# Hybrid layer with attention and pooling: pooling channels in another order, inputs of embedding, heads and gates asked for at other products, pooling operands made in two groups

## The chip, the cores and the metric

The kernel runs on one core of a Trainium2 chip. The metric is the time of one execution on the device in microseconds (us); lower is better. An execution is profiled by the hardware, and the profile's span leaves out a little at the start and the end. The engines are PE (matrix products), DVE (vector), ACT (scalar, activations), POOL and SP; SP, ACT and POOL also ask for transfers (DMA), each in its own order.

## What is computed

One decoder layer over 1024 tokens of width 2048, in f32. A projection gives queries, keys, values, two gates and the pooling channels. Sliding-window attention with 16 heads and a multi-scale pooling mixer are each multiplied by a SiLU gate, joined, and sent through one output projection. A gated embedding of p is added before the norm.

```
h = jnp.einsum('bsd,dc->bsc', x, w_in) + b_in
q, k, v, g_attn, u_pool, g_pool = jnp.split(h, SPLIT_POINTS, axis=-1)
a = banded_sink_attention(q, k, v, sinks, bias_hqk, valid) * jax.nn.silu(g_attn)
b = multiscale_pool(u_pool, w_pool, pool_scale) * jax.nn.silu(g_pool)
mix = jnp.einsum('bsc,cd->bsd', jnp.concatenate([a, b], axis=-1), w_out)
ple = jax.nn.sigmoid(jnp.einsum('bsd,de->bse', x, w_gate_ple)) * jnp.einsum('bsp,pd->bsd', p_i, w_ple)
return layer_norm(DEEPNORM_ALPHA * x + mix + ple, ln_gain, ln_bias)
```

The pooling has four channel groups 0 to 3, with trailing windows of 2, 4, 8 and 16 tokens: the mean over the window, less the token, then a 256 x 256 map per group (w_pool) and a scale.

## The kernel before

**Products.** A job is two blocks of 128 output columns over 1024 tokens. It is worked out by seven products in place of eight (p1 to p7, Strassen's way), on sums and differences of quarters of the weight and of the token operand. Every f32 operand is split into a high and a low part, and mm3 (L176) makes three matmuls of each step: high by high, high by low, low by high. A product is four such steps, 12 matmuls of 128 x 512. Weights arrive raw by SP (`raw`, a ring of five), DVE makes the sums, ACT casts the high part (L222, `wh`), DVE subtracts for the low part (`wl`), four products ahead of their use. The operand of the tokens (`b11`, `b21`, `t1` to `t4`, `b22`, each with an h and an l tile) is made once per stage by split_unit (L240: ACT L248, then DVE). Results leave the two banks qa and qb of PSUM by an ACT copy (L346) or a DVE add into `part`. Slots of a rotating pool (`s`) hold what is fetched beside.

**Stages.** s1 and s2 are the first and second half of the inner width for query, key and value columns, and s2 goes on with all others, whose partial sums go to memory. s3 takes the other half of the width for these others: gate and pooling channel pairs (gp, u) in turn, one attention gate pair, eight pairs of the embedding's gate (wgate), three attention gate pairs. s4 multiplies the pooled half by w_out, s5 the attended half, s6 the last 256 tokens. In each stage the first two and the last two jobs run side by side, products in turn (BESIDE, 14 products), the others alone (ALONE, 7 products).

**What sets the order.** A tick is one product. `after(n, fn)` (L155) writes fn's instructions into the program n ticks on, `later(n, fn)` the same but also behind the last marked result of PE, ACT or DVE. The order on each engine is therefore the order in which the program writes, and each engine and each of the DMA queues of SP, ACT and POOL takes its instructions in that order.

**What the change touches.**
- heads (L473): one head and token half per 9 ticks beside s2's products. begin fetches the query and the bias (SP), split makes the query's parts (ACT L485, L487, DVE), score makes the scores (PE L506), then softmax, share, value, shift and trans.
- pool_u (L608): window sums of a channel block by doubling, on DVE: 1, 2, 3 or 4 adds per half for groups 0 to 3, with a scalar_tensor_tensor and a split behind. After the second block it fetches the group's w_pool and the pooling gates (sgp), and mix (L640) makes 24 matmuls into banks sc, multiplied on DVE (L652) and stored by POOL to cc.
- embed_in (L656) fetches four tiles of p one per two ticks, and splits them after nine (ACT L668, DVE); embed_w (L672) fetches a pair of w_ple and splits it (ACT L150).
- gate_ahead (L592) fetches the attention result `pre` of a gate block, gate_attn (L595) applies silu and multiplies.
- set_from (L255) makes a stage's token operands from memory: begin and each step ask for tiles `two` (ACT's queue, L267), and step i makes operand i, the first as b11, b21, t1, t2 and so on.

Of the kernel before, what the change touches and what calls it, by code (L numbers as in the profile page):

```python
# [32 lines left out]
T = 512  # L33
# [7 lines left out]
Q0, KB, VB, GA0, U0, GP0 = 0, 8, 9, 10, 18, 26  # L41
# [22 lines left out]
class Layer:  # L64
# [405 lines left out]
    def heads(self, h, j):  # L470
        nc, g = self.nc, j // 4
# [21 lines left out]
        def score(bq):  # L493
            sc[bq] = self.slot()[:, :T].rearrange("p (e k) -> p e k", e=2)
            ps = self.bank("sc", 2, (P, 2, 256))
            z = k0(bq)

            if bq:
                win = [(h, (bq - 1) * P, 0, 2 * P)]
            else:  # L500
                win = ([(0, 3 * P, 0, P)] if h else []) + [(h, 0, P, P)]
            for e in range(2):
                q = qs[e][:, bq * P : (bq + 1) * P]
                for hh, o, at, n in win:
                    for i, kk in enumerate(self.kk[hh]):
                        nc.tensor.matmul(ps[:, e, at : at + n], q, kk[:, o : o + n], start=i == 0, stop=i == 1)  # L506
            for e in range(2):
                nc.vector.tensor_tensor_reduce(
                    out=sc[bq][:, e, z:], in0=ps[:, e, z:], in1=bias[0][:, e, z:], op0=ALU.add, op1=ALU.max, scale=1.0,
                    scalar=self.c(C_SINK + 8 * j + 2 * bq + e), accum_out=mx[:, 2 * bq + e : 2 * bq + e + 1])  # L510

        def shift(bq):
            f = slice(2 * bq, 2 * bq + 4)
            nc.vector.tensor_scalar(out=neg[:, f], in0=mx[:, f], scalar1=-1.0, scalar2=None, op0=ALU.mult)
            self.tt(sk[:, f], self.c(C_SINK + 8 * j + 2 * bq, 4), neg[:, f], ALU.add)
            nc.scalar.activation(sk[:, f], sk[:, f], AF.Exp)
# [14 lines left out]
        def share(bq):  # L531
            cur = sc[bq][:, :, P:]
            for e in range(2):
                i = 2 * bq + e
                nc.scalar.activation(cur[:, e], cur[:, e], AF.Copy, scale=rec[:, i : i + 1])
# [44 lines left out]
        self.later(3, split)  # L580
        for bq in range(4):
            t = 4 * (bq // 2)
            self.after(4 + 2 * bq, lambda bq=bq: score(bq))
            if bq % 2:
                self.after(8 + t, lambda bq=bq: shift(bq - 1))
                self.after(14 + t, lambda bq=bq: trans(bq - 1))
            self.after(9 + t, lambda bq=bq: softmax(bq))
            self.later(11 + t, lambda bq=bq: share(bq))
            self.after(19 + t + bq % 2, lambda bq=bq: value(bq))


    def gate_ahead(self, j):  # L592
# [15 lines left out]
    def pool_u(self, j, c):  # L608
        nc, g = self.nc, j // 2
        w = 2 << g  # L610
        out = []
        for h in range(2):
            u = self.slot()
            if h == 0:
                nc.gpsimd.memset(u[:, 0:16], 0.0)
            else:
                self.ident_act(u[:, 0:16], c[:, 0, T - 16 :], self.c(C_BIN + U0 + j))
            self.ident_act(u[:, 16:], c[:, h], self.c(C_BIN + U0 + j))
            cur, d, first = u, 1, 1
            while d < w:  # L620
                nxt = self.slot()
                end = 2 * d == w
                f = 16 if end else first
                self.tt(nxt[:, f:], cur[:, f:], cur[:, f - d : T + 16 - d], ALU.add)
                cur, d = nxt, 2 * d
                first = first + d
            if h == 0:
                self.tt(cur[:, 16 : 16 + 16], cur[:, 16 : 16 + 16], self.c(C_HEAD + 16 * g, 16), ALU.mult, nc.gpsimd)
            nc.vector.scalar_tensor_tensor(out=cur[:, 16:], in0=cur[:, 16:], scalar=1.0 / w, in1=u[:, 16:],
                                           op0=ALU.mult, op1=ALU.subtract)  # L630
            out.append(self.split(cur[:, 16:], 2 * (j % 2) + h < 3))
        self.diff[j] = out
        if j % 2:
            f = slice((g % 2) * T, (g % 2) * T + T)
            self.after(4, lambda: self.got.update({("wp", g): self.fetch(self.wpool[g // 2][:, f])}))
            self.later(8, lambda: self.got.update({("wp", g): self.split(self.got["wp", g])}))
            self.after(8, lambda: self.got.update({("sg", g): [[self.fetch(self.sgp[2 * g + e][:, h * T : h * T + T]) for e in range(2)] for h in range(2)]}))
            self.later(10, lambda: self.mix(g))

    def mix(self, g):  # L640
# [183 lines left out]
    def run(self):  # L824
# [23 lines left out]
        win, wgate, wout = self.win, self.wgate, self.wout  # L848
        pairs = lambda b, n: [(b + 2 * i, b + 2 * i + 1) for i in range(n)]
# [2 lines left out]
        store = lambda w: hid if w is win else gat  # L852
        qkv = [(win, *p) for p in [(KB, VB)] + pairs(Q0, 4)]
        ga, gp, u = ([(win, *p) for p in pairs(b, 4)] for b in (GA0, GP0, U0))
        rest = [j for two in zip(gp, u) for j in two] + ga[:1] + [(wgate, *p) for p in pairs(0, 8)] + ga[1:]

        def keep(where):
            return lambda b, c: self.load(where[b], flat(c))
# [52 lines left out]
        n2, n3, n4, n5 = (len(s) - 2 for s in (s2, s3, s4, s5))  # L911
# [81 lines left out]
        self.after(5, lambda: build_kv(KB, self.k_build, 0))  # L993
        self.after(6, lambda: build_kv(VB, self.v_build, 0))
        for i in range(16):
            self.after(t - 1 + 9 * i, lambda i=i: self.heads(i % 2, i // 2))
        self.after(t + 63 + 8, lambda: build_kv(KB, self.k_build, 1))
        self.after(t + 63 + 22, lambda: build_kv(VB, self.v_build, 1))
        self.centre_weights(8, 3)
# [9 lines left out]
        for i in range(n3):  # L1009
            if i == 1:  # L1010
                over.close()
                over = ExitStack()
                self.extras = self.work_pool("e2", 6, over)
            if self.groups[g + i + 1][0][0].b[0] == 0 and i < n3 - 1:
                self.after(1, self.embed_in)
                self.after(4, lambda: self.embed_w(0))
            if i == n3 - 1:

                over.close()
                work.close()  # L1020
                work = ExitStack()
                self.slot_n = T
                self.slots = self.work_pool("slots1", 6, work)
                self.twos = self.work_pool("twos1", 8, work)
                pooled()
                for n, b in enumerate(b for j in s3[-2:] for b in j.b):
                    self.after(4 + n, lambda b=b: self.gate_ahead(b - GA0))
            self.run_group(g + i, () if i else steps)
        g += n3

# [33 lines left out]
        for i in range(n4):  # L1064
            if i == 1:
                work.close()
                work = ExitStack()
                self.twos = self.work_pool("twos2", 8, work)
                p6.extend(5 * [pp] + [self.work_pool("p6", 1, work)])
                d0 = self.work_pool("d0", 4, work)  # L1070
            if i == n4 - 2:
                attended()
            self.run_group(g + i, () if i else make_pooled, renew if i == n4 - 1 else None)
        g += n4


# [134 lines left out]
```

## Time and profile before

| | us |
|---|---|
| median of 3 runs | 1502.66 (1502.1 to 1507.54) |
| the profiled execution | 1504.51 |
| its span | 1502.8 |
| PE busy in the span | 1453.8 (97%) |
| DVE, ACT, POOL busy | 1119.7, 781.1, 278.9 |

Lines of the profile read: L179 is line 179 of the kernel; in a row of the timeline stand start, length, engine, line, operation, what is written `<-` what is read, the shape, a count, and in brackets how long the engine was idle before and what released it. In a list of waits stand the engine and what waited, what it waited for, the time in all, how often, and the longest. The mean granted clock of PE over the execution was 0.989.

### The profile page before, as it was taken

Reading aid. Unit: us, or ns where it says so; the run is one execution under the profiler, and the core shown is the slowest. Engines: PE = TensorE matmul, PEld = TensorE weight load, DVE = VectorE, ACT = ScalarE, POOL = GpSimd, SP = SyncE. Lnnn points to the kernel's source line nnn. Section 1 sums busy time; section 2 is a strip of 40 time slices with the busy share of each in tenths; the row PEclk is TensorE's granted clock in tenths of the full one; section 3 lists DMA queues with packets and bytes.
Section 4 is the critical chain, followed back from the end, with each engine's and each line's share of the span. In section 5 each row is a group of like instructions: output and inputs, shape, how many; then the busy total and the mean of one; then the engine's idle time right before and its main releaser. Section 6 shows DMA issues by size and latency. Waiting matters only on the chain. (4 is left out here: it accounts for less than half of the span.)

```text
span 1502.8 us, 20461 instructions
## 1 busy us (share of the span) xinstructions
PE 1453.8 (97%) x6972; PEld 1225.5 (82%) x6972; DVE 1119.7 (75%) x2030; ACT 781.1 (52%) x1550; POOL 278.9 (19%) x388
## 2 busy tenths in 40 slices
PE   8999999999999999999999998999998999999986
PEld 6788888888878888888887786888886888899985
DVE  7788678888787877888675695556558866987785
ACT  5464566666666656566633353333337433555484
POOL 0000123332333332231111111000001111111241
PEclk9999999999999999999999999999999999999998
DMA  7563875445445555557766667575768678586564
GB/s 262 202 218 101 250 208 178 140 167 174 166 168 176 174 193 180 172 182 245 189 158 175 180 155 240 160 207 160 206 189 270 150 193 236 140 239 134 153 230 143
DMA packets 101721, 280.38 MB, mean 187 GB/s; under 512 B 11632, under 2 KB 16880, under 8 KB 101616
## 3 DMA queue, kind: packets, MB, share of 16 engines
q1 hardware_dynamic: 76400, 199.89, 39.9%
q0 software_dynamic: 19712, 67.64, 19.6%
q10 hardware_dynamic: 5504, 11.54, 2.3%
q8 instruction: 55, 0.90, 0.2%
q14 instruction: 50, 0.41, 0.1%
HBM read 193.04 MB, written 85.98 MB: 186 GB/s over the span
## 5 line engine op out<-in xcount | busy, mean ns | idle before, releaser
L222 ACT CAST wh<-raw 128x512 fp32r<-128x512 f32 x428 | 264.1, 620 | 450.8 <-PE qa L180 143.2
L122 DVE TENSOR_TENSOR wl<-raw,wh 128x512 fp32r<-128x512 f32 x428 | 298.2, 702 | 141.4 <-ACT wh L222 138.5
L346 ACT COPY part<-qa 128x512 f32<-128x512 f32 (+1 forms) x180 | 103.9, 577 | 54.0 <-PE qa L181 53.0
L551 POOL TENSOR_SCALAR_AFFINE_SELECT s<-s 128x512 fp32r<-128x512 f32 x128 | 101.0, 801 | 150.5 <-ACT s L544 101.1
L122 DVE TENSOR_TENSOR part<-part,qb 128x512 f32<-128x512 f32 (+1 forms) x120 | 81.0, 675 | 50.5 <-PE qb L181 47.0
L179 PE MATMUL qa<-b11h,wh 128*128 128x512 f32 (+2 forms) x292 | 110.7, 380 | 2.0 <-ACT b11h L248 1.7
L180 PE MATMUL qa<-b11l,wh 128*128 128x512 f32 (+2 forms) x292 | 109.5, 375 | 0.2 <-DVE b11l L122 0.2
L181 PE MATMUL qa<-b11h,wl 128*128 128x512 f32 (+2 forms) x292 | 109.0, 374 | 0.4 <-DVE wl L122 0.4
L179 PE MATMUL qb<-b21h,wh 128*128 128x512 f32 (+2 forms) x292 | 109.3, 374 | 0.0
L181 PE MATMUL qb<-b21h,wl 128*128 128x512 f32 (+2 forms) x292 | 108.9, 373 | 0.0
L180 PE MATMUL qb<-b21l,wh 128*128 128x512 f32 (+2 forms) x292 | 108.7, 372 | 0.0
L179 PE MATMUL qb<-t1h,wh 128*128 128x512 f32 (+1 forms) x260 | 102.1, 393 | 4.3 <-DVE part L122 2.9
L179 PE MATMUL qa<-t2h,wh 128*128 128x512 f32 (+1 forms) x260 | 100.6, 388 | 3.5 <-ACT wh L222 3.5
L179 PE MATMUL qa<-t3h,wh 128*128 128x512 f32 (+1 forms) x260 | 100.9, 388 | 3.1 <-ACT part L346 3.1
L181 PE MATMUL qb<-t1h,wl 128*128 128x512 f32 (+1 forms) x260 | 101.1, 389 | 1.5 <-DVE wl L122 1.5
L181 PE MATMUL qa<-t2h,wl 128*128 128x512 f32 (+1 forms) x260 | 100.0, 385 | 1.5 <-DVE wl L122 1.5
L180 PE MATMUL qb<-t1l,wh 128*128 128x512 f32 (+1 forms) x260 | 100.9, 388 | 0.0
L179 PE MATMUL qa<-t4h,wh 128*128 128x512 f32 (+1 forms) x260 | 100.4, 386 | 0.3 <-DVE part L122 0.3
L179 PE MATMUL qb<-b22h,wh 128*128 128x512 f32 (+1 forms) x260 | 100.4, 386 | 0.0
L180 PE MATMUL qa<-t4l,wh 128*128 128x512 f32 (+1 forms) x260 | 99.7, 383 | 0.0
L181 PE MATMUL qa<-t4h,wl 128*128 128x512 f32 (+1 forms) x260 | 99.7, 383 | 0.0
L180 PE MATMUL qa<-t3l,wh 128*128 128x512 f32 (+1 forms) x260 | 99.7, 383 | 0.0
(286 smaller groups left out, 3568.9 us busy)
## 6 DMA issues: line engine op xcount, KB each, us to landing
raw<-in_win SPq DMA_DIRECT2D x65, 512.0 KB, 4.2
h<-part SPq DMA_DIRECT2D x34, 512.0 KB, 2.9
part<-h POOLq DMA_DIRECT2D x34, 512.0 KB, 6.0
cw<-in_wout SPq DMA_DIRECT2D x64, 256.0 KB, 3.1
raw<-in_wgate SPq DMA_DIRECT2D x32, 512.0 KB, 4.1
raw<-wc SPq DMA_DIRECT2D x32, 512.0 KB, 4.4
s<-in_x SPq DMA_DIRECT2D x44, 256.0 KB, 5.3
wc<-cw SPq DMA_DIRECT2D x32, 256.0 KB, 2.3
```

Source lines behind the costliest of these rows:

```text
L122: return (eng or self.nc.vector).tensor_tensor(out=out, in0=a, in1=b, op=op)
L179: mm(ps, wh, xh, start=start, stop=False, skip_group_check=True)
L180: mm(ps, wh, xl, start=False, stop=False, skip_group_check=True)
L181: return mm(ps, wl, xh, start=False, stop=stop, skip_group_check=True)
L222: self.unit_latest = [nc.scalar.copy(out=hi, in_=src).ins, L.lo(lo, src, hi).ins]
L346: self.mark("ACT", self.nc.scalar.copy(out=dst, in_=ps))
L551: nc.gpsimd.affine_select(out=o4, in_=a4, pattern=[[0, 4], [sign, P]], compare_op=ALU.is_ge, fill=0.0, base=0 if side else -1, channel_mul ...
```

## The change

Five things move, and no instruction changes its kind or size. The heads begin one tick earlier, and all their steps but the fetch and the split keep their place. The pooling groups follow each other as 0, 3, 2, 1 in place of 0, 1, 2, 3, and the pooling gates are fetched two ticks earlier. The four fetches of p begin four ticks later, the first w_ple three ticks later. The pooling operands of s4 are made in s3's last group from tick 10 on, every second tick, in place of s4's first group; the stage's first job needs them from tick 14 on. The `pre` of the last gates are fetched from tick 9 in place of tick 4. In the changed kernel the lines from L1027 on have numbers higher by two.

```diff
--- before.py
+++ after.py
@@ -580,13 +580,13 @@
         self.later(3, split)
         for bq in range(4):
             t = 4 * (bq // 2)
-            self.after(4 + 2 * bq, lambda bq=bq: score(bq))
+            self.after(5 + 2 * bq, lambda bq=bq: score(bq))
             if bq % 2:
-                self.after(8 + t, lambda bq=bq: shift(bq - 1))
-                self.after(14 + t, lambda bq=bq: trans(bq - 1))
-            self.after(9 + t, lambda bq=bq: softmax(bq))
-            self.later(11 + t, lambda bq=bq: share(bq))
-            self.after(19 + t + bq % 2, lambda bq=bq: value(bq))
+                self.after(9 + t, lambda bq=bq: shift(bq - 1))
+                self.after(15 + t, lambda bq=bq: trans(bq - 1))
+            self.after(10 + t, lambda bq=bq: softmax(bq))
+            self.later(12 + t, lambda bq=bq: share(bq))
+            self.after(20 + t + bq % 2, lambda bq=bq: value(bq))
 
 
     def gate_ahead(self, j):
@@ -634,7 +634,7 @@
             f = slice((g % 2) * T, (g % 2) * T + T)
             self.after(4, lambda: self.got.update({("wp", g): self.fetch(self.wpool[g // 2][:, f])}))
             self.later(8, lambda: self.got.update({("wp", g): self.split(self.got["wp", g])}))
-            self.after(8, lambda: self.got.update({("sg", g): [[self.fetch(self.sgp[2 * g + e][:, h * T : h * T + T]) for e in range(2)] for h in range(2)]}))
+            self.after(6, lambda: self.got.update({("sg", g): [[self.fetch(self.sgp[2 * g + e][:, h * T : h * T + T]) for e in range(2)] for h in range(2)]}))
             self.later(10, lambda: self.mix(g))
 
     def mix(self, g):
@@ -852,7 +852,7 @@
         store = lambda w: hid if w is win else gat
         qkv = [(win, *p) for p in [(KB, VB)] + pairs(Q0, 4)]
         ga, gp, u = ([(win, *p) for p in pairs(b, 4)] for b in (GA0, GP0, U0))
-        rest = [j for two in zip(gp, u) for j in two] + ga[:1] + [(wgate, *p) for p in pairs(0, 8)] + ga[1:]
+        rest = [j for two in ((gp[g], u[g]) for g in (0, 3, 2, 1)) for j in two] + ga[:1] + [(wgate, *p) for p in pairs(0, 8)] + ga[1:]
 
         def keep(where):
             return lambda b, c: self.load(where[b], flat(c))
@@ -993,7 +993,7 @@
         self.after(5, lambda: build_kv(KB, self.k_build, 0))
         self.after(6, lambda: build_kv(VB, self.v_build, 0))
         for i in range(16):
-            self.after(t - 1 + 9 * i, lambda i=i: self.heads(i % 2, i // 2))
+            self.after(t - 2 + 9 * i, lambda i=i: self.heads(i % 2, i // 2))
         self.after(t + 63 + 8, lambda: build_kv(KB, self.k_build, 1))
         self.after(t + 63 + 22, lambda: build_kv(VB, self.v_build, 1))
         self.centre_weights(8, 3)
@@ -1012,8 +1012,8 @@
                 over = ExitStack()
                 self.extras = self.work_pool("e2", 6, over)
             if self.groups[g + i + 1][0][0].b[0] == 0 and i < n3 - 1:
-                self.after(1, self.embed_in)
-                self.after(4, lambda: self.embed_w(0))
+                self.after(5, self.embed_in)
+                self.after(7, lambda: self.embed_w(0))
             if i == n3 - 1:
 
                 over.close()
@@ -1023,8 +1023,10 @@
                 self.slots = self.work_pool("slots1", 6, work)
                 self.twos = self.work_pool("twos1", 8, work)
                 pooled()
+                for n, step in enumerate(make_pooled):
+                    self.after(10 + 2 * n, step)
                 for n, b in enumerate(b for j in s3[-2:] for b in j.b):
-                    self.after(4 + n, lambda b=b: self.gate_ahead(b - GA0))
+                    self.after(9 + n, lambda b=b: self.gate_ahead(b - GA0))
             self.run_group(g + i, () if i else steps)
         g += n3
 
@@ -1070,7 +1072,7 @@
                 d0 = self.work_pool("d0", 4, work)
             if i == n4 - 2:
                 attended()
-            self.run_group(g + i, () if i else make_pooled, renew if i == n4 - 1 else None)
+            self.run_group(g + i, then=renew if i == n4 - 1 else None)
         g += n4
```

The order on three queues shows it. First the heads, on DVE: at a head in s2, the rows about the low parts of the query (`s` of 64x512; `wl` are low parts of weights). Before:

```order
L122 TENSOR_TENSOR s_4492<-pv_4451,s_4493 64x256 x2
L122 TENSOR_TENSOR wl_4504<-s_915_4464,wh_4503 128x512
L122 TENSOR_TENSOR wl_4535<-raw_4064,wh_4534 128x512
L122 TENSOR_TENSOR s_4528<-s_4402,s_4528 64x512
L122 TENSOR_TENSOR s_4529<-s_4402,s_4529 64x512
L122 TENSOR_TENSOR st_4066<-st_4066 128x2
L122 TENSOR_TENSOR part_4501<-part_4501,qb_4538 128x512
```

and now:

```order
L122 TENSOR_TENSOR s_4492<-pv_4451,s_4493 64x256 x2
L122 TENSOR_TENSOR s_4501<-s_4374,s_4501 64x512
L122 TENSOR_TENSOR s_4502<-s_4374,s_4502 64x512
L122 TENSOR_TENSOR wl_4510<-s_915_4464,wh_4509 128x512
L122 TENSOR_TENSOR wl_4535<-raw_4069,wh_4534 128x512
L122 TENSOR_TENSOR st_4036<-st_4036 128x2
L525 RECIPROCAL st_4036<-st_4036 128x2
```

The two query rows stood behind the two weight rows, and now stand ahead of them.

Second the queue of SP at the passage from the pooling channels to the gates of the embedding (`raw` are gate weights, `in_p` and `in_wple` the embedding's inputs, `pre` the attention result, `in_wpool` the last pooling group's weight). Before:

```order
L136 DMA raw_8592<-in_wgate 128x1024
L136 DMA raw_8678<-in_wgate 128x1024
L136 DMA raw_8815<-in_wgate 128x1024
L136 DMA raw_8859<-in_wgate 128x1024
L136 DMA s_8680<-in_wple 128x512
L136 DMA s_8682<-in_p 128x512
L136 DMA s_8718<-in_p 128x512
L136 DMA s_8747<-pre_154 128x512
L136 DMA s_8749<-pre_154 128x512
L136 DMA s_8752<-pre_155 128x512
L136 DMA s_8754<-pre_155 128x512
L136 DMA s_8756<-in_wpool 128x512
```

and now:

```order
L136 DMA raw_8606<-in_wgate 128x1024
L136 DMA raw_8676<-in_wgate 128x1024
L136 DMA s_8712<-in_p 128x512
L136 DMA s_8737<-pre_154 128x512
L136 DMA s_8739<-pre_154 128x512
L136 DMA s_8742<-pre_155 128x512
L136 DMA s_8744<-pre_155 128x512
L136 DMA s_8746<-in_wple 128x512
L136 DMA s_8748<-in_wpool 128x512
L136 DMA s_8770<-in_p 128x512
L136 DMA s_8790<-sgp_164 128x512
L136 DMA s_8792<-sgp_165 128x512
```

Before, four loads of raw weights stand ahead of in_wple, in_wpool and the second in_p (the first in_p stands ahead of them all); now two do, and the others come behind.

Third DVE where s3 ends and s4 begins (`two`, `t1l`, `t2l` are pooling operands, `raw`, `s`, `wl` weights, `part<-s` the attention result times its gate, and `part<-qb` the add that frees a bank of PSUM). Before, the last 12 rows up to that add:

```order
L122 TENSOR_TENSOR raw_10680<-raw_10375,raw_10680 128x512
L122 TENSOR_TENSOR wl_10844<-s_2129_10838,wh_10843 128x512
L122 TENSOR_TENSOR raw_10375<-s_2129_10838,raw_10375 128x512
L122 TENSOR_TENSOR part_10484<-s_10586,part_10484 128x512
L122 TENSOR_TENSOR part_10484<-s_10588,part_10484 128x512
L122 TENSOR_TENSOR part_10485<-s_10612,part_10485 128x512
L122 TENSOR_TENSOR part_10485<-s_10614,part_10485 128x512
L122 TENSOR_TENSOR raw_10375<-raw_10375 128x512
L122 TENSOR_TENSOR two_10506<-two_10655,two_10506 128x1024
L122 TENSOR_TENSOR two_10507<-two_10656,two_10507 128x1024
L122 TENSOR_TENSOR s_2135_10877<-raw_10718 128x512
L122 TENSOR_TENSOR part_10794<-part_10794,qb_10886 128x512
```

and now:

```order
L122 TENSOR_TENSOR wl_10852<-s_2131_10846,wh_10851 128x512
L122 TENSOR_TENSOR raw_10375<-s_2131_10846,raw_10375 128x512
L122 TENSOR_TENSOR t2l_10870<-two_10507,t2h_10869 128x1024
L122 TENSOR_TENSOR raw_10375<-raw_10375 128x512
L122 TENSOR_TENSOR two_10604<-two_10643,two_10604 128x1024
L122 TENSOR_TENSOR two_10605<-two_10644,two_10605 128x1024
L122 TENSOR_TENSOR part_10486<-s_10737,part_10486 128x512
L122 TENSOR_TENSOR part_10486<-s_10739,part_10486 128x512
L122 TENSOR_TENSOR part_10487<-s_10766,part_10487 128x512
L122 TENSOR_TENSOR part_10487<-s_10768,part_10487 128x512
L122 TENSOR_TENSOR s_2137_10885<-raw_10706 128x512
L122 TENSOR_TENSOR part_10816<-part_10816,qb_10894 128x512
```

Before, the gate products of part_10484 and part_10485 and one pair of differences stand in the rows ahead of the add; now t2l, a further pair of differences and the gate products of part_10486 and part_10487 stand ahead of it as well, which came behind it before. From the first `b11l` to this add there are 28 rows before and 36 now.

## The prediction

> **What bounds the kernel now.** I read the page first, for the span and the busy shares.
>
> ```profile
> span 1502.8 us, 20461 instructions
> PE 1453.8 (97%) x6972; PEld 1225.5 (82%) x6972; DVE 1119.7 (75%) x2030; ACT 781.1 (52%) x1550; POOL 278.9 (19%) x388
> ```
>
> PE is busy for 1453.8 of 1502.8 us, so all its idle time is 49 us, and the change removes no matmul. It can only shorten or lengthen those 49 us, and the stretches in which PE runs at a lower granted clock. The list of waits, filtered to PE, says whom PE waits for: the time in all, how often, the longest.
>
> ```profile
> PE sc L179 <- ACT s L150: 5.3, 1, 5.3
> PE sc L506 <- DVE s L122: 5.2, 11, 1.2
> PE qa L179 <- ACT part L346: 3.1, 1, 3.1
> PE qb L179 <- DVE part L122: 2.9, 3, 1.0
> ```
>
> One wait at a pooling product is 5.3 us, eleven at head scores are 5.2 together, and one at a product of the last group is 3.1. A table of windows then shows where busy time (the first pair: length, PE busy) and the granted clock (the column before the DMA share) fall off.
>
> ```profile
> 450.00:500.00 50.00, 49.32 (x249) 41.19 (x249) 40.72 (x99) 29.71 (x76) 17.27 (x22) 1.00 0.55 181
> 900.00:950.00 50.00, 44.72 (x183) 36.13 (x182) 28.41 (x44) 18.14 (x28) 4.66 (x8) 0.93 0.72 222
> 1100.00:1150.00 50.00, 46.91 (x207) 38.43 (x206) 33.82 (x48) 25.29 (x37) 6.37 (x8) 1.00 0.83 247
> 1150.00:1200.00 50.00, 46.61 (x196) 37.56 (x195) 44.10 (x59) 25.54 (x38) 7.52 (x12) 0.97 0.60 158
> ```
>
> The heads lose little per window; 900 to 950 (the passage from pooling to gates) and 1100 to 1200 (the last s3 group and the first s4 group) lose most, and two of them lose clock too. The change works at these three places, in the order of the queues.
>
> **1. Heads one tick earlier.** Every head's score stays where it was among the products; its query fetch and split move one tick forward. The timeline of one head, PE first, then DVE:
>
> ```profile
> 448.60 0.33 PE L506 MATMUL sc<-kh,s 128*128 128x128 f32 x1 [1.21 <-DVE s L122]
> 446.06 0.69 DVE L122 TENSOR_TENSOR wl<-s,wh 128x512 fp32r<-128x512 f32 x1 [0.84 <-ACT wh L222]
> 446.68 0.69 DVE L122 TENSOR_TENSOR wl<-raw,wh 128x512 fp32r<-128x512 f32 x1
> 447.86 1.40 DVE L122 TENSOR_TENSOR s<-s,s 64x512 fp32r<-64x512 f32 x2 [0.49 <-ACT s L485]
> ```
>
> The two low parts of the query stand behind two weight splits on DVE; in the new order they stand ahead of them (rows above, in the section on the change). That is 2 x 0.6 us sooner, where the wait was 1.21. The weight splits that go back are for products further on, so PE does not wait there. The order moves low parts past a weight split in 10 of the 16 heads, so I take 10/16 of 5.2: **-3.3** (from -1 to -5.2).
>
> **2. Embedding inputs asked for later, pooling order 0, 3, 2, 1.** The 5.3 us wait, by engine: PE, ACT, then SP.
>
> ```profile
> 907.43 0.80 PE L179 MATMUL sc<-e,s 128*128 128x512 f32 x1 [5.28 <-ACT s L150]
> 906.24 0.62 ACT L668 CAST s<-s 128x512 fp32r<-128x512 f32 x1 [6.33 <-DMA s<-in_p]
> 906.76 0.61 ACT L150 CAST s<-s 128x512 fp32r<-128x512 f32 x1
> 862.08 26.69 SPq L136 DMA_DIRECT2D raw<-in_wgate  x4
> 864.57 0.33 SPq L136 DMA_DIRECT2D raw<-in_wgate  x1
> 889.33 0.86 SPq L136 DMA_DIRECT2D s<-in_p  x2
> 890.29 2.15 SPq L136 DMA_DIRECT2D s<-pre  x4
> 893.30 0.33 SPq L136 DMA_DIRECT2D s<-in_wpool  x1
> ```
>
> The pooling weight's cast (906.76) is what PE waits for, but ACT had stood 6.33 us before the embedding input's cast ahead of it, and that input was asked for at 889.33. SP had been held since 864.57 behind raw gate weights that wait for buffers, with wple, p, pre and wpool queued behind. PE's loss goes on after the gap:
>
> ```profile
> 906.80:913.60 6.80, 6.17 (x15) 4.82 (x16) 3.29 (x5) 6.01 (x9) 0.54 (x1) 0.50 0.98 369
> ```
>
> In that window the clock is 0.50 for 6.17 busy us, so 3.1 us are lost, and the place costs 5.28 + 3.1 = 8.4. In the new order only two raw gate weights stand ahead of p, pre, wple and wpool, and ACT's casts of wple and wpool stand ahead of all four embedding casts. If slots are free, wpool goes out soon after the second raw weight, 864.57 + 0.43 + 2.15 + 0.33, about 868. From 893.30 to 906.76 is 13.5 us at most for landing and cast, so it is ready by about 882. The mix stands 45 matmuls earlier on PE (at 1453.8 / 6972 = 0.209 us each 9.4 us), so PE is there at 907.43 - 5.28 - 9.4 = 892.8. The stall goes with 10 us to spare. I leave 0.5, the mean of a head-score wait (5.2 / 11), for what is late next: **-7.9** (from 0 to -8.4).
>
> The first pooling products have a smaller wait of the same kind (DVE, then PE):
>
> ```profile
> 801.23 0.75 DVE L652 SCALAR_TENSOR_TENSOR s<-sc,cst,s 128x512 f32<-128x512 f32 x1 [2.00 <-DMA s<-sgp]
> 802.04 0.50 PE L179 MATMUL sc<-e,s 128*128 128x512 f32 x1 [1.37 <-DVE s L652]
> ```
>
> The gate there lands late; it is now asked for two ticks sooner. Against it, group 3 with 24 adds instead of group 1's 16 now comes second, with its pooling weight behind the gate stores on SP. 1.37 may go and as much may come; taken **-1** (from -3 to +3).
>
> **3. Pooling operands made in the last s3 group, gates fetched five ticks later.** Two stalls lie here. The first:
>
> ```profile
> 1130.35 0.50 PE L179 MATMUL qa<-t3h,wh 128*128 128x512 f32 x1 [3.09 <-ACT part L346]
> 1116.19 4.28 ACTq L267 DMA_DIRECT2D two<-cc  x4
> 1116.35 7.76 SPq L136 DMA_DIRECT2D s<-pre  x6
> 1128.18 0.62 ACT L222 CAST wh<-raw 128x512 fp32r<-128x512 f32 x1 [7.04 <-DMA two<-cc]
> ```
>
> ACT stands 7.04 us because a transfer that it is to issue waits for the landing of an earlier one, and PE's bank waits for ACT. SP was held up to 1116.35 by its own earlier waits, so five later ticks in the program do not move the six pre loads much; ACT's order there is the same. **-0.5** (from -3 to +1). [...]
>
> The second (PE, then DVE):
>
> ```profile
> 1158.82 0.47 PE L179 MATMUL qb<-t1h,wh 128*128 128x512 f32 x1 [0.98 <-DVE part L122]
> 1163.44 0.50 PE L179 MATMUL qa<-t2h,wh 128*128 128x512 f32 x1 [1.38 <-ACT wh L222]
> 1164.96 0.50 PE L179 MATMUL qb<-t1h,wh 128*128 128x512 f32 x1 [1.02 <-DVE part L122]
> 1135.81 1.22 DVE L122 TENSOR_TENSOR b11l<-two,b11h 128x1024 fp32r<-128x1024 f32 x1
> 1152.10 2.50 DVE L122 TENSOR_TENSOR part<-s,part 128x512 f32<-128x512 f32 x4
> 1155.11 2.36 DVE L122 TENSOR_TENSOR two<-two,two 128x1024 f32<-128x1024 f32 x2
> 1157.98 0.69 DVE L122 TENSOR_TENSOR part<-part,qb 128x512 f32<-128x512 f32 x1
> 1135.80:1165.00 29.20, 25.81 (x113) 20.49 (x111) 29.07 (x41) 20.20 (x27) 5.69 (x8) 1.00 0.82 242
> 1166.00:1169.60 3.60, 3.60 (x10) 2.83 (x9) 3.60 (x5) 0.55 (x2) 0.00 (x0) 0.53 0.00 0
> ```
>
> DVE is busy 29.07 of 29.20 us (the third number of the window's row), so here its order is the time. PE waits 0.98 + 1.38 + 1.02 = 3.4, then runs 3.6 us at a clock of 0.53, which loses 1.7: 5.1 in all. From the first b11l (1135.81) to the add that frees bank qb (1157.98) DVE does 28 operations: 10 of 1024 columns and 18 of 512. One of 1024 takes 1.14 (two end after 2.36, one alone after 1.22), one of 512 takes 0.603 (four in 2.50, one alone 0.69): 11.4 + 10.9 = 22.3, against 22.17 in the trace. In the new order 36 stand between the same two: 14 of 1024 and 22 of 512, for t2l, the next differences and the second pair of gate products now stand ahead of the add. That is 16.0 + 13.3 = 29.2, so the add starts at 1165.0, and PE, which followed it by 0.84, starts at 1165.85. PE is there at 1158.82 - 0.98 = 1157.84: a stall of 8.0. After a gap of 5.28 PE lost 3.1 to the clock, and I take the same here. So 8.0 + 3.1 = 11.1 in place of 5.1: **+6.0** (from -5.1, if nothing waits there any more, to +9).
>
> [...]
>
> **The sum.** -3.3 - 7.9 - 1 - 0.5 + 6.0 = -6.7 us. The profiled execution took 1504.51 us, 1.71 more than its span, and would take 1497.8. The median of the three runs, 1502.66, lies 1.85 below the profiled execution, so the forecast is 1496.0. 0.5%, 7.5 us, is about what a measurement of this kernel can tell from no change.
>
> **The rivals.**
> *Operands made earlier are a gain.* The order of DVE is the program's, but it could run ahead where the ACT casts it follows are early, and with the operands out of the way the waits at 1158 to 1165 go. Against it: 29.07 of 29.20. For it: the work is moved away from the stage in which PE waits for DVE. With -5.1 in place of +6.0 the sum is -17.8: 1484.9; with nothing there, -12.7: 1490.0. It decides if eight fewer operations precede the add.
> *The 907 stall stays.* If slots are not free, SP stands as long at p as it did at raw. For it: the pooling differences hold slots of the same pool up to the mix. Against: 10 us to spare, and the last group before the gates now has 16 adds where it had 24. Then +1.2: 1503.9.
> *SP is blocked in the heads (slower).* The fetch of a query one tick earlier asks for a slot one tick earlier. SP serves in order, so if the slot is not free, the raw weights behind it go late.
>
> ```profile
> SPq L136 <- DVE wl L122: 607.9, 130, 28.3
> SPq L136 <- PE pv L564: 2.3, 2, 1.7
> ```
>
> Slot waits (the second row) are small now, and a raw load waits 607.9 / 130 = 4.7 us for its own buffer on average. A hold under 4.7 us is therefore absorbed; one over it makes PE wait. Priced at the longest score wait, 1.2 us, for each of 16 heads it is +19.2 in place of -3.3: +15.8, 1518.5.
> *Nothing moves.* SP and the rings hold everything to its old times: 1502.7.
>
> **How the numbers follow.** Forecast 0.45 (its own range 1492 to 1500, of which 0.18 is under 1495.2 and 0.27 within 0.5%); earlier operands a gain 0.25 (all faster); the stall stays 0.12 and nothing moves 0.06 (both the same); SP blocked 0.12 (slower). So faster 0.43, same 0.45, slower 0.12. The range from 1487 to 1504 leaves out the last case and the lower third of the second, 0.20.
>
> **What would show it.** Right: score waits (L506) under 2.5 us in all; at the mix before the gates no wait over 1 us and a clock of 1.00 in 900 to 950; at the first t1 product of s4's second job a wait of 7 to 9 us behind a DVE add, with a clock under 1 after it. Wrong: that wait under 2 us (the operands' term), wpool asked for after 885 (the pooling term), or raw loads of the heads landing late with PE behind wl.

## The result, and the profile after

The changed kernel took 1498.75 us (median of 7 runs, 1493.15 to 1499.8) beside 1503.23 us for the kernel before (7 runs, 1501.15 to 1507.76): a ratio of 0.995 with a 95% interval of 0.9927 to 0.9973. A second group of runs gave 0.994 (0.9918 to 0.9962). The profiled execution took 1499.8 us with a span of 1498.1, 4.7 us under the span before.

The list of waits of the changed kernel, filtered to PE (who waited for whom, the time in all, how often, the longest):

```profile
PE qb L179 <- ACT wh L222: 9.7, 2, 9.1
PE qa L181 <- DVE wl L122: 6.7, 6, 2.7
PE qa L179 <- ACT part L346: 3.5, 2, 2.9
PE tr L457 <- DVE s L122: 1.6, 1, 1.6
PE qb L179 <- DVE part L122: 0.9, 1, 0.9
```

The 5.3 us before the embedding's gates and the eleven waits at head scores are not in the list any more. In their place stands one wait of 9.1 us, and a wait at L457, the build of the values, has grown from 0.4 to 1.6. The windows of the changed kernel:

```profile
450.00:500.00 50.00, 48.35 (x247) 40.63 (x247) 41.59 (x101) 31.64 (x82) 16.64 (x22) 1.00 0.52 180
900.00:950.00 50.00, 50.00 (x220) 41.02 (x219) 29.99 (x47) 18.68 (x30) 3.48 (x4) 1.00 0.64 169
1100.00:1150.00 50.00, 44.60 (x189) 36.09 (x187) 33.40 (x45) 28.00 (x39) 5.78 (x8) 0.97 0.81 249
1150.00:1200.00 50.00, 43.45 (x183) 35.88 (x184) 38.43 (x51) 21.51 (x33) 6.99 (x11) 0.90 0.56 153
```

The row of 450 to 500 is the one that got worse among the heads (48.35 us busy, 49.32 before): the L457 wait lies in it. From 900 to 950 PE is busy throughout at full clock, where it was 44.72 us at 0.93. From 1150 to 1200 it lost 3.2 us more than before, and the clock went from 0.97 to 0.90.

To say what each part is worth, the span is cut at rows that both kernels have: the first head score, the last product with the values, the first pooling product, the last embedding product, and the first column sum of the norm (L797). These rows of the changed kernel's timeline are:

```profile
186.24 0.22 PE L506 MATMUL sc<-kh,s 128*128 128x128 f32 x1
693.94 0.64 PE L564 MATMUL pv<-s,v 128*128 128x256 f32 x4
751.69 0.39 PE L179 MATMUL sc<-e,s 128*128 128x512 f32 x1
1092.58 0.39 PE L181 MATMUL sc<-e,s 128*128 128x512 f32 x1
1429.19 0.28 PE L797 MATMUL pv<-ones,sq 128*128 128x1 f32 x2
```

and of the kernel before:

```profile
182.75 0.22 PE L506 MATMUL sc<-kh,s 128*128 128x128 f32 x1
695.64 0.63 PE L564 MATMUL pv<-s,v 128*128 128x256 f32 x4
753.41 0.39 PE L179 MATMUL sc<-e,s 128*128 128x512 f32 x1
1104.39 0.40 PE L181 MATMUL sc<-e,s 128*128 128x512 f32 x1
1434.11 0.28 PE L797 MATMUL pv<-ones,sq 128*128 128x1 f32 x2
```

| us | before | changed | difference |
|---|---|---|---|
| up to the first score (of the change, only the first head's fetch and split lie there) | 182.8 | 186.2 | +3.5 |
| first score to last value: the heads | 512.9 | 507.7 | -5.2 |
| first pooling to last embedding product: the pooling | 351.0 | 340.9 | -10.1 |
| from there to the column sum: the operands | 329.7 | 336.6 | +6.9 |

The changed stretches together are worth -8.4 in this pair. The first stretch, which the change hardly reaches, took 3.5 back: at 41 us PE waited 2.72 us in this execution and went on at half clock, and 1.08 before with full clock behind it. That is a matter of the execution (last section).

### The profile page after: what moved, and what is told of

It is laid out like the page before. It is cut to its first block, busy times and chain, and to the rows that moved or that the text cites. A ratio compares the mean times of both kernels' runs of the same rounds, so it can differ in the third digit from the quotient of the medians.

```text
span 1498.1 us, 20465 instructions
## 1 busy us (share of the span) xinstructions
PE 1450.5 (97%) x6972; PEld 1225.3 (82%) x6972; DVE 1121.1 (75%) x2030; ACT 781.2 (52%) x1550; POOL 278.6 (19%) x388
## 5 line engine op out<-in xcount | busy, mean ns | idle before, releaser
L180 PE MATMUL qa<-t2l,wh 128*128 128x512 f32 (+1 forms) x260 | 100.5, 387 | 0.0
L181 PE MATMUL qa<-t3h,wl 128*128 128x512 f32 (+1 forms) x260 | 100.2, 386 | 0.0
```

The source lines that it names most:

```text
L180: mm(ps, wh, xl, start=False, stop=False, skip_group_check=True)
L181: return mm(ps, wl, xh, start=False, stop=stop, skip_group_check=True)
```

## The experiments

Every kernel was timed beside the kernel before. The table has the ratio, and the same three stretches of each profiled execution:

| kernel | ratio to before, 95% interval | heads | pooling | operands |
|---|---|---|---|---|
| before | 1 | 512.9 | 351.0 | 329.7 |
| changed | 0.995 (0.9927 to 0.9973) | 507.7 | 340.9 | 336.6 |
| e1 operands back in s4 | 0.9909 (0.989 to 0.9927) | 509.2 | 341.1 | 330.2 |
| e2 heads alone | 0.9964 (0.9949 to 0.9979) | 509.3 | 349.6 | 329.3 |
| e3 pooling part alone | 0.9935 (0.9917 to 0.9953) | 511.1 | 340.5 | 332.7 |
| e4 operands part alone | 1.0046 (1.0032 to 1.006) | 512.1 | 349.9 | 338.4 |
| e5 pooling order alone | 0.9938 (0.9916 to 0.9959) | 512.1 | 340.5 | 332.7 |
| e6 embedding's timing alone | 0.9996 (0.9983 to 1.0009) | 512.3 | 351.8 | 327.6 |
| e7 operands one product later | 0.9932 (0.9911 to 0.9954) | 509.5 | 340.4 | 332.7 |
| e8 two operands early | 0.9926 (0.9907 to 0.9946) | 509.1 | 341.0 | 332.1 |
| e9 e1, values one product later | 0.991 (0.9889 to 0.9931) | 510.9 | 340.7 | 329.7 |
| e10 e1, values two later | 0.9878 (0.9855 to 0.99) | 505.2 | 341.2 | 332.1 |
| e11 e1, gates as before | 0.9899 (0.9879 to 0.9919) | 507.5 | 341.5 | 329.8 |
| e12 changed, again | 0.994 (0.9918 to 0.9962) | 507.0 | 340.4 | 336.3 |

### The parts: e1 to e4

e1 takes the operands' move out of the changed kernel:

```diff
-                for n, step in enumerate(make_pooled):
-                    self.after(10 + 2 * n, step)
-            self.run_group(g + i, then=renew if i == n4 - 1 else None)
+            self.run_group(g + i, () if i else make_pooled, renew if i == n4 - 1 else None)
```

> The changed kernel with the pooling operands made in s4's first group again, all else as changed (the gates' inputs still asked for at tick 9). Theory (the vector engine's order): the 9.1 us wait at the first t1 product of s4's second job goes back to waits of about 3.4 us in all and 1.7 us lost to the clock, so about 6 us less than the changed kernel: about 1492.5 beside 1498.75. Rival (the gates' inputs asked for five ticks later make ACT late, and ACT is the one named as releaser): the wait of about 9 us stays, and the time is that of the changed kernel.

Measured: 1491.98 us, 0.9909. The wait at the first t1 product of s4's second job is 2.79 us, again behind the add:

```profile
1146.41 0.76 PE L179 MATMUL qb<-t1h,wh 128*128 128x512 f32 x1 [2.79 <-DVE part L122]
1153.11 0.50 PE L179 MATMUL qa<-t2h,wh 128*128 128x512 f32 x1 [0.81 <-ACT wh L222]
```

The operands stretch is 6.4 us shorter than in the changed kernel, with the gates' inputs still late. The move of the operands costs this, and the later gates do not.

e2 is the kernel before with the seven numbers of heads and its begin changed (`score` at 5 + 2 bq in place of 4 + 2 bq and so on, begin at t - 2).

> The kernel before with the earlier heads alone. Theory: from the first head score to the first pooling product 5.2 us less than before, so about 1498 beside 1503; the waits for the query's low part go, one wait of 1 to 2 us at a head stays. Rival (SP blocked by slots in the heads): waits behind raw weights, the same or slower than before. Rival (the idle that the profile shows in the heads is all there was to win): 2.7 us, about 1500.5.

Measured: 0.9964, 1499.94 us; the heads' stretch is 509.3 against 512.9. That is 3.6 us (to the first pooling product as well), where the theory gave 5.2 and the second rival 2.7; the ratio says 5.4, from 3.2 to 7.7. Which of the two is nearer is not settled by this run. No wait for the query's low part is left in the list, and one wait at L457 took 2.5 us. Two lines of the list:

```profile
PE sc L179 <- ACT s L150: 6.5, 1, 6.5
PE tr L457 <- DVE s L122: 2.5, 1, 2.5
```

The last line is new in size: 0.41 before. The rival of a blocked SP falls, since the stretch is shorter and no wait on weights of that size took its place.

e3 is the kernel before with the pooling order, the earlier pooling gates and the later inputs of the embedding.

> The kernel before with the pooling order 0, 3, 2, 1, the gates of the pooling fetched two ticks earlier, and the embedding's inputs fetched later, alone. Theory: the 5.3 us wait ahead of the embedding's gates and the half clock behind it go, with the small waits at 802 to 850: 10 us from the first pooling product to the last embedding product, about 1493 beside 1503. Rival (the wait went because of the other parts): it stays, about 1502.

Measured: 0.9935; the pooling stretch is 340.5 against 351.0, and no wait over 0.25 us stands before the embedding's gates.

e4 is the kernel before with the operands made in the last s3 group and the later gates.

> The kernel before with the earlier pooling operands and the later gate inputs alone. Theory (the vector engine's order): a wait of about 9 us at the first t1 product of s4's second job, then some microseconds at half clock, 6 to 7 us more than before: about 1509.5 beside 1503. Rival (the wait hangs on what came before it, so on the other parts): no more than 2 us of wait there, about 1503.

Measured: 1.0046, 1512.26 us, slower. The wait is there without the other parts:

```profile
1167.13 0.76 PE L179 MATMUL qb<-t1h,wh 128*128 128x512 f32 x1 [10.08 <-ACT wh L222]
```

The three parts add up: -0.36 - 0.65 + 0.46 = -0.55% where the whole gave -0.5 and -0.6%.

### Which half of the pooling part: e5 and e6

e5 keeps the order of groups and the earlier gates of the pooling:

```diff
-        rest = [j for two in zip(gp, u) for j in two] + ...
+        rest = [j for two in ((gp[g], u[g]) for g in (0, 3, 2, 1)) for j in two] + ...
```

> The kernel before with the pooling order 0, 3, 2, 1 and the earlier fetch of the pooling gates alone; the embedding's inputs are asked for as before. Theory (SP's queue: with the new order only two raw gate weights stand ahead of the embedding's inputs and the last pooling weight): the wait ahead of the embedding's gates falls from 5.3 us to under 1, and 8 to 10 us are saved, about 0.994 of before. Rival (the later asking of the embedding's inputs is what frees ACT): 4 us of wait or more stay, and the gain is under 4 us.

e6 keeps the later inputs of the embedding:

```diff
-                self.after(1, self.embed_in)
-                self.after(4, lambda: self.embed_w(0))
+                self.after(5, self.embed_in)
+                self.after(7, lambda: self.embed_w(0))
```

> The kernel before with the later fetches of the embedding's inputs alone; pooling order as before, so four raw gate weights still stand ahead of the pooling weight on SP, but ACT casts the pooling weight ahead of the embedding's inputs. Theory (SP's queue): the pooling weight is still asked for near 890, and 2 to 5 us of wait stay ahead of the embedding's gates; 0 to 4 us are saved, about 0.998 of before. Rival (ACT's order alone): the wait is under 1 us, and 8 us are saved, about 0.994.

Measured: e5 0.9938, e6 0.9996. The order, with the earlier gates of the pooling, is all of the gain; the later inputs alone bring nothing. The order and those gates were not tried apart. In e5 no wait is left at the mix, although ACT still casts an embedding input (885.34) ahead of the pooling weight (886.10). SP passes the raw weights (the first row is the second of the two) and asks for the pooling weight at 873.10:

```profile
861.03 0.33 SPq L136 DMA_DIRECT2D raw<-in_wgate  x1
861.45 0.38 SPq L136 DMA_DIRECT2D s<-in_wple  x1
862.94 1.54 SPq L136 DMA_DIRECT2D s<-in_p  x2
867.69 3.91 SPq L136 DMA_DIRECT2D s<-pre  x4
873.10 0.33 SPq L136 DMA_DIRECT2D s<-in_wpool  x1
```

In e6 (PE, then SP, then ACT) four raw weights hold SP for 26.67 us as before:

```profile
906.05 0.79 PE L179 MATMUL sc<-e,s 128*128 128x512 f32 x1 [6.08 <-ACT s L150]
863.31 26.67 SPq L136 DMA_DIRECT2D raw<-in_wgate  x4
893.21 0.49 SPq L136 DMA_DIRECT2D s<-in_wpool  x1
905.38 0.62 ACT L150 CAST s<-s 128x512 fp32r<-128x512 f32 x1 [1.76 <-DMA s<-in_wpool]
```

The pooling weight's cast now does stand ahead of the embedding's casts, and still waits: the weight itself, asked for at 893.21, is not there before 905.38. I had expected 2 to 5 us of wait here; it was 6.08, because a landing took 12 us at that time. In the kernel before, the weight had landed at 903.76 and its cast stood behind ACT's embedding cast until 906.76; in e6 ACT was free for it, and it landed only at 905.35. ACT's order was not what counted; what counted was when SP could ask.

### The vector engine's order as a dose: e7 and e8

e7 makes the operands one product later, e8 only the first two early:

```diff
-                    self.after(10 + 2 * n, step)
+                    self.after(11 + 2 * n, step)
```

```diff
-                    self.after(10 + 2 * n, step)
+                    self.after(10 + 2 * n if n < 2 else 12 + 2 * n, step)
```

> The changed kernel with the pooling operands one product later (from tick 11 on). A dose between two known ones: from the first b11l to the add that frees bank qb the vector engine has 36 rows in the changed kernel (29.2 us by the durations), 28 with the operands in s4 (22.2 us), and here 36 of which three fewer are of 1024 columns (27.6 us). Theory (the vector engine's order): a wait of 9.1 - 1.6 = 7.5 us there, and a time 1 to 2 us under the changed kernel, about 0.994 of before. Rival (what counts is whether the operands are made before the group's end or not): the wait goes back to under 3.5 us, and the time is that with the operands in s4, about 0.991.

> The changed kernel with only the first two pooling operands (b11, b21) made early, the others one pair of products later, as in s4's first group. By the durations 22.2 us of vector work stand between the first b11l and the add, as with all operands in s4. Theory (the vector engine's order): the wait is 2 to 3.5 us, the time that with the operands in s4, about 0.991 of before, or up to 2 us better. Rival (any operand made in the last s3 group delays what the last products need): 9 us of wait, 0.995.

Measured, from the start of the first b11l to the start of the add, with the operands stretch beside it:

| kernel | by the durations | in the trace | PE's waits at the t1 and t2 products there | stretch |
|---|---|---|---|---|
| before | 22.2 | 22.17 | 0.98 + 1.38 + 1.02 | 329.7 |
| e8 two early | 22.2 | 23.40 | 2.17 + 1.12 + 1.07 | 332.1 |
| e7 one product later | 27.6 | 27.54 | 3.33 + 2.28 | 332.7 |
| changed | 29.2 | 30.66 | 9.10 | 336.6 |

The two waits of e7 and the first of e8:

```profile
1146.27 0.50 PE L179 MATMUL qa<-t2h,wh 128*128 128x512 f32 x1 [3.33 <-ACT wh L222]
1149.29 0.80 PE L179 MATMUL qa<-t2h,wh 128*128 128x512 f32 x1 [2.28 <-ACT wh L222]
```

```profile
1150.96 0.47 PE L179 MATMUL qb<-t1h,wh 128*128 128x512 f32 x1 [2.17 <-DVE part L122]
```

The count of vector work holds in each (within 1.5 us; e4, which has all operands early too, took 31.30 for 29.2). The waits follow it, but not to the size I had given for e7: 5.6 us in two places in place of 7.5 in one, and 3.9 us less than the changed kernel in the stretch where I had said 1 to 2. In e7 the product that waits is another one (t2, for a weight), so part of the vector work that comes late seems to be out of PE's way; this was not tried apart. e7's rival, under 3.5 us and the time of operands in s4, holds no better: e7's waits and its ratio lie between. In e8 the wait is in the range of the theory, and the rival of 9 us falls. No arrangement with early operands beats making them in s4: the nine profiles with that have 327.6 to 332.7 us in this stretch, and e7 and e8 lie at its upper end.

### What the heads still lost: e9 and e10

e9 and e10 are e1 with one number more, 23 and 24:

```diff
-        self.after(t + 63 + 22, lambda: build_kv(VB, self.v_build, 1))
+        self.after(t + 63 + 24, lambda: build_kv(VB, self.v_build, 1))
```

> The changed kernel with the pooling operands in s4's first group again, and the second build of the values one product later (tick 23 of its row in place of 22). In the runs with earlier heads PE waited 1.65 to 2.81 us at this build's transposes, 0.41 before: the earlier heads left nine matmuls between a head's transpose and the build's in the one bank that both use, where 18 stood before. Theory (the earlier heads' gain is cut by this one wait): the wait falls under 1 us, and 1.5 to 2.5 us are saved against operands in s4 alone, about 0.9895 of before. Rival (the vector engine is late there whatever stands in that bank): the wait moves to another place and nothing is saved, 0.991.

> The same with the second build of the values two products later (tick 24). Theory: as with one product later, the wait under 0.5 us, about 0.9893 of before. Rival: the wait moves on, to the scores or the head's own transposes, 0.991.

Measured: e9 0.991 with its wait unchanged,

```profile
470.97 0.66 PE L457 MATMUL tr<-ident,s 128*128 128x128 f32 x4 [2.45 <-DVE s L122]
```

and e10 0.9878 with no wait at that build over 0.25 us. So the distance in the bank alone does not explain the wait: e9 restored the 18 matmuls that the kernel before had, and PE waited as long; with e10's 34 it did not wait. The row that PE waits for is the DVE subtraction that empties the bank: in e9 it ends 6.1 us after the last of the head's transposes began, before 4.3. Why it comes later was not tried apart and stays open. e10's heads take 505.2, the shortest of all, and it is the fastest kernel of the study: its interval lies below those of both the kernel before and the changed one, and overlaps those of e1, e9 and e11.

### The gates, and the changed kernel again: e11 and e12

e11 takes back the gates' later inputs as well (tick 4 in place of 9); e12 is the changed kernel.

> The changed kernel with the pooling operands in s4's first group and the last gates' inputs asked for at tick 4 again, as before; only the heads, the pooling order and the embedding's inputs are changed. Theory (the later gates are worth next to nothing): within 1.5 us of the kernel with operands in s4 and later gates, about 0.991 of before, the ACT wait near 1116 at 2.5 to 4 us as in both. Rival (the later gates free the transfers): 2 to 3 us slower than that, 0.993.

> The changed kernel itself, beside the kernels of this group, for a second profile. Theory (the half clock at 41 us is a chance of the execution): the same wait of about 2.7 us at the first t2 product, or 1.08, and the time up to the first head score either near 182.5 or near 185 to 186 us, with all else as in the first profile: a wait of 9 us at the first t1 product of s4's second job. Rival (the start is slower by the change): 186 again and in every run of this kernel. Time 0.995 of before.

Measured: e11 0.9899, e1 0.9909, their intervals overlapping, and the ACT wait at 1117.60 is 2.96 us. The later gates are worth nothing that can be told. e12 gave 0.994, and its start differs from the first profile of the same kernel:

```profile
1151.07 0.77 PE L179 MATMUL qb<-t1h,wh 128*128 128x512 f32 x1 [8.69 <-ACT wh L222]
```

The wait for the operands is there again, while its first score stands at 182.8 us in place of 186.2, so the rival of a slower start falls.

## Why the prediction was right

The forecast was 1496.0 in a range of 1487 to 1504, and the median 1498.75; in the ratio, 6.7 us less of 1503 is 0.9955, and 0.995 and 0.994 were measured. The sum was made of terms of both signs, and each that can be told came out with its sign:

| term | forecast | measured |
|---|---|---|
| heads | -3.3 | -3.6 (seven profiles with the new heads and the values built as before, 508.5 in the mean; five without, 512.1) |
| pooling, both places | -7.9 and -1 | -9.8 (ten profiles with the new order, 340.8 in the mean; four without, 350.6) |
| gates' inputs later | -0.5 | nothing that can be told (e11 beside e1) |
| operands | +6.0 | +6.4 (changed beside e1), +6.1 (e12 beside e1), +8.7 (e4 beside before) |

**Heads.** The step held as written: the low parts stand ahead of the weight splits, and the eleven waits went. The share taken, 10 of 16 heads, gave the right size by luck. The waits in the list went whole (5.2), and more than the list shows: score rows are shown 0.28 us long but follow each other after 0.11, so a wait between two of them is counted from the end of the first. From row to row, without the listed waits, all score rows take 35.4 to 35.5 us in the five profiles without the new heads and 33.0 to 33.6 in the nine with them. Against that 1.2 to 2.4 us came back at the build of the values (L457), which the prediction had not looked at, and in five of the eight profiles with that wait the clock was halved for 3.4 us behind it, which cost 1.4 to 1.7 more. That the earlier fetch would block SP, the slower rival, did not happen.

**Pooling.** SP's queue was the cause as argued, with the pooling weight asked for at 866.95 (about 868 forecast), cast by 885.8 (about 882), and PE at the mix at 887.53 (892.8 forecast). SP, ACT and PE of the changed kernel:

```profile
860.35 0.33 SPq L136 DMA_DIRECT2D raw<-in_wgate  x1
866.95 0.41 SPq L136 DMA_DIRECT2D s<-in_wpool  x1
884.62 1.14 ACT L150 CAST s<-s 128x512 fp32r<-128x512 f32 x2
887.53 0.40 PE L179 MATMUL sc<-e,s 128*128 128x512 f32 x1
```

PE comes 5 us sooner than forecast, and of the 10 us to spare 2 were left. The bound of 13.5 us for landing and cast did not hold, for another reason: the weight had landed at 870.58, 3.6 us after it was asked for, and ACT, busy without a gap just before, cast it in its turn. Without waits over 0.1 us and without the time lost to the clock, the pooling stretch is 338.2 to 338.6 us in all fourteen profiles; with the old order 9.4 to 10.4 us of waits and 1.6 to 3.1 of clock come on top, with the new 2.2 to 3.0 and none. The prediction drew on both halves of this part at once, though, and put ACT's new order of casts beside SP's: e5 shows that the order of the groups, with the earlier pooling gates, does it without the rest, and e6 that the later inputs, and with them the casts' order, do nothing alone.

**Operands.** The vector engine's count was the term that turned the sum, and it held best. In the changed kernel (DVE, then ACT, then PE):

```profile
1125.06 1.22 DVE L122 TENSOR_TENSOR b11l<-two,b11h 128x1024 fp32r<-128x1024 f32 x1
1143.95 1.29 DVE L122 TENSOR_TENSOR part<-s,part 128x512 f32<-128x512 f32 x2 [1.13 <-ACT part L597]
1155.12 0.69 DVE L122 TENSOR_TENSOR s<-raw 128x512 f32<-128x512 f32 x1
1155.72 0.68 DVE L122 TENSOR_TENSOR part<-part,qb 128x512 f32<-128x512 f32 x1
1155.84 0.62 ACT L222 CAST wh<-s 128x512 fp32r<-128x512 f32 x1 [1.96 <-DVE s L122]
1156.55 0.77 PE L179 MATMUL qb<-t1h,wh 128*128 128x512 f32 x1 [9.10 <-ACT wh L222]
1156.60:1165.00 8.40, 8.40 (x29) 6.79 (x30) 8.40 (x11) 3.66 (x7) 0.20 (x1) 0.76 0.21 81
```

From b11l to the add it takes 30.66 us; 29.2 were forecast, and 1.13 of the rest is a wait for ACT's silu. The wait is 9.10 where 8.0 was forecast. The profile names ACT's cast as the releaser and not the add: the cast of a weight sum, which DVE wrote in the row just ahead of the add, ended last. Both hang in the same queue, so the place and the cause were right and the name of the last releaser was not; the sign named beforehand, 7 to 9 us behind a DVE add, was met but for that name and 0.1 us. The clock then lost 8.4 x 0.24 = 2.0 us where 3.1 were taken, from a gap of 5.28 that cost that much elsewhere. 9.1 + 2.0 = 11.1 is the forecast's figure, by two errors that cancel: that is luck. Without waits and clock losses the stretch is 319.5 to 321.1 us in all fourteen profiles. Waits take 5.7 to 9.2 us with the operands in s4 and 12.8 to 14.3 in the three with all of them early, the clock 1.7 to 4.6 and 3.8 to 4.5; so the move costs 5.8 us of waits and 1.7 of clock in the mean.

The rival that earlier operands would be a gain had a chance of 0.25. e1 and e4 speak against it from both sides.

## What to carry to other kernels

An engine that is busy without a gap over some tens of microseconds can be planned by counting: add up what stands ahead of the operation that others wait for, in the new order, by the durations of the trace (here 29.2 us counted and 30.66 taken). Work taken out of a busy stretch and put at its start is not taken out, and what was behind the releasing operation now stands in front of it (PE's wait there grew from 0.98 to 9.10 us). When a load arrives late, look at what its queue was held by when it was written in the program, and move that: asking later, behind the same holder, changed nothing here (e6, 0.9996, with SP held for 26.67 us as before). And try parts apart: this change held a gain of 1% and a loss of half that.

## What the runs showed of the hardware

The clock after a wait is a matter of the execution. All fourteen profiles run the same program up to the first head, and PE waits there for a weight's low part, 1.08 to 1.12 us in four of them and 2.68 to 2.72 in ten. (In the four, PE had been at half clock for 3.4 us from about 32 us on, and came to this place later by what the wait is shorter: 1.64 us in the kernel before against the changed one, counted from DVE's rows.) The row of the changed kernel, its window, and the window of e1 after the same wait (2.69):

```profile
41.82 0.79 PE L181 MATMUL qa<-t2h,wl 128*128 128x512 f32 x1 [2.72 <-DVE wl L122]
41.00:48.00 7.00, 6.18 (x15) 4.83 (x16) 7.00 (x9) 2.26 (x4) 0.00 (x0) 0.51 0.47 187
```

```profile
40.99 0.50 PE L181 MATMUL qa<-t2h,wl 128*128 128x512 f32 x1 [2.69 <-DVE wl L122]
41.00:48.00 7.00, 7.00 (x31) 5.80 (x32) 7.00 (x9) 3.89 (x7) 0.00 (x0) 1.00 0.47 188
```

PE does 15 matmuls in the one and 31 in the other. Of the ten with a wait of 2.7, two ran the window at 0.51, three at 0.76 and five at 1.00. The first head score stands at 186.2 us in the first two, at 184.5 to 185.2 in the next three, and in the five at 182.3 to 182.9 but for one, e11, which waited 1.54 us more at the first build of the values.

The traces show what the clock goes with. Between 12 and 1470 us, every stretch at half clock lies a whole number of steps of 3.413 us (the shortest such stretch in the clock records of the traces) from every other of its trace and is one to four such steps long (in the kernel before they begin at 32.95, 906.77, 1166.18 and 1456.31 us, the later ones 256, 332 and 417 steps after the first). Cut into these steps, PE's idle time in one step, as the rows of the trace show it, goes with the clock of the next. After a step at full clock with 1.87 us of idle or more the next was at half in all 34 cases; with 1.0 to 1.57 us in none of 94; between the two in 8 of 18. (Below 1.0 it was so in four of 5746, all near 1430 us where PE does not wait; that stays open.) After a step at half clock the next stayed at half with 0.66 us of idle or more (17 cases) and was full with 0.56 or less (47). So the same wait costs clock where most of it falls into one step, as in the changed kernel,

```profile
37.73:41.14 3.41, 1.37 (x7) 0.79 (x5) 3.41 (x5) 2.15 (x3) 0.00 (x0) 1.00 0.09 35
41.14:44.55 3.41, 2.73 (x7) 2.15 (x8) 3.41 (x6) 1.05 (x1) 0.00 (x0) 0.50 0.69 273
```

and none where a boundary divides it, as in e1 (1.40 and 1.28 us idle):

```profile
36.29:39.70 3.41, 2.01 (x9) 1.31 (x7) 3.41 (x5) 1.57 (x3) 0.00 (x0) 1.00 0.01 2
39.71:43.12 3.41, 2.13 (x9) 1.78 (x10) 3.41 (x5) 1.61 (x2) 0.00 (x0) 1.00 0.77 308
```

In the kernel before, the same reading covers both places at which the prediction looked: the 3.09 us at 1130 fell into two steps with 1.38 and 1.71 us of idle and cost no clock, and the short gaps ahead of 1166 put 1.70 us into one step, behind which the clock was halved.

All this makes two profiles of one kernel differ by 3.4 us (186.2 and 182.8, changed and e12) before the change begins, a large part of what this change is worth. The pooling stretch, between rows that both kernels have, was steadier: in the ten profiles with the new pooling order it took 340.4 to 341.5 us. The other two were less so, 507.0 to 509.5 us in the heads of the changed order and 327.6 to 332.7 where the operands are made in s4.
